# A two-layer diffusion block on one core: the second layer's modulation summed on VectorE in place of TensorE

## The chip, the core and the metric

The kernel runs on one core of one Trainium2 chip. The metric is the device time of one execution in microseconds. A core has a tensor engine (TensorE, in the rows PE; its weight loads have a row of their own, PEld), a vector engine (VectorE, DVE), a scalar engine (ScalarE, ACT), GpSimd (POOL) and SyncE (SP), whose queue here issues nearly all transfers. Each engine works through its own instructions in order and waits for the others by semaphores.

## The reference

Two layers work on 256 latent tokens and 256 context tokens of width 1024. Ahead of each mixer and each feed-forward part the stream is normalised and modulated, and each part's result is gated. Shift, scale and gate come from the conditioning vectors, one for the latents (`c`) and one for the context (`c_ctx`):

```
silu_c  = silu(c);  silu_cc = silu(c_ctx)
m_lat = split(silu_c  @ mod_w[i] + mod_b[i], 6)      # mod_w[i]: 1024 x 6144
m_ctx = split(silu_cc @ mod_w[i] + mod_b[i], 6)
z_lat = modulate(rmsnorm(x, norm1_g[i]), m_lat[0], m_lat[1]) @ w_in[i]
x = x + m_lat[2] * merge(z_lat, att_lat)
x = x + m_lat[5] * ffn(modulate(rmsnorm(x, norm2_g[i]), m_lat[3], m_lat[4]))
```

The feed-forward part is a dense SwiGLU of width 2816 in layer 0 and eight experts, two per token, in layer 1. In the last layer the context only feeds the mixer, so of its modulation only shift and scale of the first norm (`m_ctx[0]`, `m_ctx[1]`) are used.

## The kernel before

**Stages.** Activations lie transposed, 128 features on the partitions and the tokens along the free axis. The order in time is: filters, conditioning and the first modulation (to about 60 us of the profile), mixer of layer 0 with its output projection (to about 320), the dense SwiGLU of layer 0 (to about 710), mixer of layer 1 (to about 870), the experts. A weight block for a matrix multiplication is loaded as 128x1024 floats (`raw`), rounded by ScalarE to `wh` (L262), and VectorE keeps the remainder `wl` (L263). A product is made of three matmuls (L272 to L274), so a block over 512 tokens is 24 matmuls of 128x512 (18 in the last part of the dense stage). `wh` and `wl` have four buffers each, `mm` in PSUM has three, and `raw` has seven, which the modulation's weights (`modw`, tag `raw`, L345) share.

**The modulation** is a vector times a 1024 x 6144 matrix, cut into 12 tiles of 512 output columns (`ct`) for each layer; a tile comes in four chunks (`q`) of 256 rows. For a chunk, `modulation_part` makes four small matmuls (L353): the weights are 32 columns wide (`cvec`: the two conditioning vectors, rest zero) and each goes to its own 32 columns of the array, with 256 columns of `modw` streamed past:

```
for k in range(2):
    for n in range(2):
        g = 64 * k + 32 * n
        self.nc.tensor.matmul(ps[g:g + 32, :L], self.cvec[:, 2 * q + k], w[:, ...], start=q == 0, stop=q == 3, tile_position=(0, g))
```

After the fourth chunk `modulation_row` copies the result out on ScalarE (L360), turns it with two transposes on TensorE (L363), adds its halves on VectorE (L367) and adds the bias (L369). The result is `modT[l]`, with 48 column blocks for both streams.

**Where the chunks stand.** Ten tiles of layer 0 are made in the mixer. The list `chunks` holds the rest: two tiles of layer 0 and all twelve of layer 1, each chunk by itself. `mod_chunk` takes one off the list. It is called in `dense` after each gate or up block but the first three, and in `add_blocks` after each block of the first two of the three parts of the down projection: one chunk after a block of 24 matmuls. The scheduler of the language orders instructions within engines by their dependences from this program order.

**Around it.** Gate times up is made on ScalarE (L890) and VectorE (L891) and split into two parts by `split` (L266, L267); the down projection's result is added to the stream by VectorE in `residual` (L839, once for the latents and once for the context).

Of the kernel before, what the change touches and what calls it, by code (L numbers as in the profile page):

```python
# [18 lines left out]
F32 = mybir.dt.float32  # L19
# [3 lines left out]
OP = mybir.AluOpType  # L23
AX = mybir.AxisListType

P = 128
D = 1024
KD = D // P
L = 256
# [8 lines left out]
PAD = 8  # L38
# [157 lines left out]
class Trunk:  # L196
# [130 lines left out]
    def conditioning(self):  # L327

        nc = self.nc
        lo = self.par_at["c"][0]  # L330
        both = self.pars[:, lo:lo + 2 * KD]
        sc = self.keep.tile([P, 2 * KD], F32, name="silu_c")
        nc.scalar.activation(sc, both, AF.Exp, scale=-1.0)
        nc.vector.tensor_scalar(sc, sc, 1.0, None, op0=OP.add)
        nc.vector.reciprocal(sc, sc)
        nc.vector.tensor_mul(sc, sc, both)
        self.cvec = self.pre.tile([P, KD, 32], F32, name="cvec")
        nc.gpsimd.memset(self.cvec, 0.0)
        for j in range(2):
            nc.vector.tensor_copy(self.cvec[:, :, j], sc[:, j * KD:(j + 1) * KD])  # L340
# [51 lines left out]
    def mod_chunk(self):  # L392

        if not self.chunks:
            return
        l, ct, q = self.chunks.pop(0)
        if q == 0:
            self.mod_ps = self.sc()
        self.modulation_part(self.mod_ps, q, self.modulation_load(l, ct, q))
        if q == 3:  # L400
            self.modulation_row(l, ct, self.mod_ps, self.aux)

    def mod_chunks_until(self, l, ct):
        while self.chunks and self.chunks[0][:2] < (l, ct):
            self.mod_chunk()
# [1037 lines left out]
```

## Time and profile before

| | |
|---|---|
| median of 3 runs | 1789.05 us (1787.66 to 1789.59) |
| the profiled execution | 1784.13 us |
| its span, first to last instruction | 1782.6 us |
| TensorE busy, share of the span | 1682.3 us, 94% |
| VectorE busy | 608.7 us, 34% |
| ScalarE busy | 445.1 us, 25% |
| GpSimd busy | 29.4 us, 2% |

A busy TensorE in these rows is one that has matmuls in flight: records overlap, and their ends are modelled. How long something takes in TensorE's queue is read from the distance of starts. "x8" in a row of the time line means that eight adjacent records were merged. An fp32 matmul leaves two records, so the four small matmuls of a chunk are eight.

### The profile page before, as it was taken

How to read it: one execution, taken by the hardware profiler on the slowest of the kernel's cores; microseconds unless marked ns; L12 is line 12 of the kernel's file. 1: busy time of each engine (PE TensorE's matmuls, PEld its weight loads, DVE VectorE, ACT ScalarE, POOL GpSimd, SP SyncE). 2: the span in 40 equal slices, each digit the busy share in tenths (PEclk: the TensorE clock that was granted, in tenths of full speed). 3: DMA queues.
4: the chain of work that ended last, by engine and by line, in shares of the span. 5: the costliest groups of instructions: out<-in, count | busy, mean ns of one | idle time of the engine just before them, and what ended most of it. 6: DMA issues, size and time to landing. Idle time of an engine off the chain costs nothing. (4 is left out here: it accounts for less than half of the span.)

```text
span 1782.6 us, 27678 instructions
## 1 busy us (share of the span) xinstructions
PE 1682.3 (94%) x11718; PEld 1087.0 (61%) x11718; DVE 608.7 (34%) x1352; ACT 445.1 (25%) x866; POOL 29.4 (2%) x38
## 2 busy tenths in 40 slices
PE   6999999999999999999889999999999999999997
PEld 3877568877777778885755554454545445444443
DVE  5655876423333324778520100311003110031103
ACT  5443564322222123546410000101001000010101
POOL 0021000000000000011000000000000000000000
PEclk9999999999999999999899999999999999999998
DMA  8521353455555553525369999989999899999996
GB/s 311 184 90 44 142 201 95 154 166 165 165 165 166 165 148 113 191 87 195 142 251 367 385 372 412 386 338 403 375 407 425 358 398 370 415 416 397 425 425 261
DMA packets 86313, 475.92 MB, mean 267 GB/s; under 512 B 9707, under 2 KB 13068, under 8 KB 43148
## 3 DMA queue, kind: packets, MB, share of 16 engines
q1 hardware_dynamic: 85580, 473.12, 69.7%
q8 instruction: 121, 1.98, 0.4%
q10 hardware_dynamic: 576, 0.52, 0.1%
q14 instruction: 36, 0.29, 0.0%
HBM read 472.55 MB, written 1.05 MB: 266 GB/s over the span
## 5 line engine op out<-in xcount | busy, mean ns | idle before, releaser
L1136 PE MATMUL mm<-mraw,xg 128*64 128x256 f32 x3584 | 409.5, 382 | 5.2 <-PEq L1192 2.3
L1136 PEld LDWEIGHTS mm<-mraw,xg 128*64 128x64 f32 x3584 | 254.3, 137 | 135.6 <-issue 9.5
L272 PE MATMUL mm<-xh,wh 128*128 128x512 f32 (+1 forms) x656 | 240.6, 368 | 0.8 <-ACT wh L262 0.4
L274 PE MATMUL mm<-xh,wl 128*128 128x512 f32 (+1 forms) x656 | 237.7, 363 | 0.3 <-DVE wl L263 0.3
L273 PE MATMUL mm<-xl,wh 128*128 128x512 f32 (+1 forms) x656 | 237.8, 363 | 0.1
L262 ACT CAST wh<-raw 128x1024 fp32r<-128x1024 f32 (+1 forms) x124 | 128.0, 1034 | 362.5 <-PE mm L273 345.8
L263 DVE TENSOR_TENSOR wl<-raw,wh 128x1024 fp32r<-128x1024 f32 (+1 forms) x124 | 150.1, 1212 | 139.6 <-ACT wh L262 137.9
L272 PEld LDWEIGHTS mm<-xh,wh 128*128 128x128 f32 x656 | 122.9, 188 | 37.2 <-issue 16.5
L274 PEld LDWEIGHTS mm<-xh,wl 128*128 128x128 f32 x656 | 123.2, 188 | 21.7 <-issue 2.2
L273 PEld LDWEIGHTS mm<-xl,wh 128*128 128x128 f32 x656 | 123.0, 188 | 18.9 <-issue 1.5
L1153 DVE TENSOR_TENSOR h<-h,mm 128x256 f32<-128x256 f32 x56 | 23.6, 422 | 320.4 <-ACT h L1152 320.4
L1185 PE MATMUL sc<-mraw,ht 128*64 128x512 f32 x448 | 109.4, 603 | 3.2 <-PEq L1192 1.4
L1185 PE MATMUL mm<-mraw,ht 128*64 128x512 f32 x448 | 108.6, 603 | 3.2 <-PEq L1192 2.1
L1152 ACT ACTIVATE h<-mm 128x256 f32<-128x256 f32 x56 | 21.5, 383 | 344.4 <-PE mm L1136 344.4
L1156 DVE TENSOR_TENSOR hx<-hx,sc 64x256 f32<-64x256 f32 x56 | 23.8, 425 | 242.4 <-ACT hx L1155 242.1
L1155 ACT ACTIVATE hx<-sc 64x256 f32<-64x256 f32 x56 | 21.0, 375 | 288.2 <-PE sc L1147 177.1
L1147 PE MATMUL sc<-mraw,xg 128*32 128x256 f32 x1344 | 76.4, 379 | 0.0
L1164 PE MATMUL aux<-tab_ident,h 128*128 128x128 f32 x112 | 25.1, 302 | 43.7 <-DVE h L1153 43.5
L1185 PEld LDWEIGHTS sc<-mraw,ht 128*64 128x64 f32 x448 | 30.3, 136 | 53.2 <-issue 40.2
L1185 PEld LDWEIGHTS mm<-mraw,ht 128*64 128x64 f32 x448 | 29.0, 136 | 53.9 <-issue 47.1
L1147 PEld LDWEIGHTS sc<-mraw,xg 128*32 128x32 f32 x1344 | 43.4, 110 | 29.2 <-issue 0.8
L1164 PEld LDWEIGHTS aux<-tab_ident,h 128*128 128x128 f32 x112 | 11.5, 140 | 70.2 <-DVE h L1153 64.5
(330 smaller groups left out, 2039.9 us busy)
## 6 DMA issues: line engine op xcount, KB each, us to landing
mraw<-in_eg_dram SPq DMA_DIRECT2D x112, 1024.0 KB, 12.1
mraw<-in_eu_dram SPq DMA_DIRECT2D x112, 1024.0 KB, 15.3
mraw<-in_ed_dram SPq DMA_DIRECT2D x112, 1024.0 KB, 8.6
modw<-in_mod_dram SPq DMA_DIRECT2D x96, 512.0 KB, 3.8
raw<-in_win_dram SPq DMA_DIRECT2D x40, 512.0 KB, 3.9
raw<-in_fg_dram SPq DMA_DIRECT2D x22, 512.0 KB, 4.5
raw<-in_fu_dram SPq DMA_DIRECT2D x22, 512.0 KB, 4.6
raw<-in_wout_dram SPq DMA_DIRECT2D x16, 512.0 KB, 4.4
```

The costliest lines, as they stand in the source:

```text
L262: nc.scalar.copy(hi, raw)
L263: nc.vector.tensor_sub(lo, raw, hi.bitcast(F32))
L272: mm(ps, w[0], x[0], start=start, stop=False)
L273: mm(ps, w[0], x[1], start=False, stop=False)
L274: mm(ps, w[1], x[0], start=False, stop=stop)
L1136: mm(pm[MAIN * j:MAIN * (j + 1), i * L:(i + 1) * L], xg[:, k, :MAIN], r, start=k == 0, stop=k == KD - 1, tile_position=(0, MAIN * j))
L1147: mm(px[q:q + EXTRA], xg[:, k, MAIN:], r, start=k == 0, stop=k == KD - 1, tile_position=(0, q))
L1152: nc.scalar.activation(h, pm[:, :L], AF.Silu)
L1153: nc.vector.tensor_mul(h, h, pm[:, L:])
L1156: nc.vector.tensor_mul(hx[64:], hx[64:], px[64:])
L1164: nc.tensor.transpose(pt[:, f], h[:, f], self.ident)
L1185: mm(pds[e % 2][n * MAIN:(n + 1) * MAIN], ht[:, c:c + MAIN], r[:, at + n * 512:at + (n + 1) * 512], start=ft == 0 and k == 0, stop=ft == N ...
```

## The change

For layer 1, `mod_chunk` calls the new function `mod_sums`. The chunk's weights are loaded as before. VectorE multiplies each half of 128x512 by a column of `silu_c` (one value per partition) and adds it to an accumulator `acc` of 128x512: the first by `tensor_scalar`, the seven others by `scalar_tensor_tensor`. There is one accumulator for the latents and, in the tiles 0 to 3, whose context part is used, one for the context; both use buffers of the tags `pz` and `pa`, which have one buffer each. After the fourth chunk TensorE sums over the partitions, with 128 columns of the accumulator as weights and one column of ones streamed past, four matmuls for an accumulator, and VectorE adds the bias from PSUM. In the tiles 4 to 11 the context's half of `modT` gets the latents' values, and nobody reads it. The matmuls of L353, the copy of L360, the transposes and the reductions are gone for layer 1. Layer 0 is as before.

```diff
+        self.silu_c = sc
...
         l, ct, q = self.chunks.pop(0)
+        if l == 1:
+            return self.mod_sums(ct, q)
         if q == 0:
             self.mod_ps = self.sc()
...
+    def mod_sums(self, ct, q):
+
+
+        nc = self.nc
+        streams = 2 if ct < 4 else 1
+        if q == 0:
+            wide = [self.temps.tile([P, 2, L + 2 * PAD], F32, name=self.name(n), tag=n, bufs=1) for n in ("pz", "pa")[:streams]]
+            self.sums = [t.rearrange("p s t -> p (s t)")[:, :512] for t in wide]
+        w = self.modulation_load(1, ct, q)
+        for k in range(2):
+            wk = w[:, k * 512:(k + 1) * 512]
+            for j, acc in enumerate(self.sums):
+                c = j * KD + 2 * q + k
+                c = self.silu_c[:, c:c + 1]
+                if q == k == 0:
+                    nc.vector.tensor_scalar(acc, wk, c, None, op0=OP.mult)
+                else:
+                    nc.vector.scalar_tensor_tensor(acc, wk, c, acc, op0=OP.mult, op1=OP.add)
+        if q == 3:
+            ps = self.aux(8)
+            for j, acc in enumerate(self.sums):
+                for b in range(4):
+                    nc.tensor.matmul(ps[:, 4 * j + b:4 * j + b + 1], acc[:, b * P:(b + 1) * P], self.ones[:, 0:1],
+                                     start=True, stop=True)
+            m, mb = self.modT[1][:, 4 * ct:4 * ct + 4], self.par("mod_b1")[:, 4 * ct:4 * ct + 4]
+            for j in range(2):
+                at = 4 * j if streams == 2 else 0
+                nc.vector.tensor_add(m[:, :, j], ps[:, at:at + 4], mb)
```

In the rows of the changed kernel, lines behind the new function have moved by 32 (L839 is L871, L891 is L923); the new ones are L421 (first product), L423 (multiply and add), L428 (sum over partitions) and L433 (bias). The transfers on SP's queue stand in the same order in both kernels, and so do all the other matmuls on TensorE.

On TensorE, at the end of the second tile of layer 1, between the last block of the up projection and the first of the down projection (`mm` is the block's result in PSUM, `hy` and `q` are parts of the hidden layer), before:

```order
L273 MATMUL mm_3636<-hy_720_3546,wh_3632 128x512
L274 MATMUL mm_3636<-hy_719_3545,wl_3633 128x512
L353 MATMUL sc_3535<-modw_3661,cvec 32x256 x4
L272 MATMUL mm_3683<-q_623_2987,wh_3679 128x512
L273 MATMUL mm_3683<-q_624_2988,wh_3679 128x512
L274 MATMUL mm_3683<-q_623_2987,wl_3680 128x512
L272 MATMUL mm_3683<-q_632_3032,wh_3679 128x512
L363 MATMUL aux_3669<-tab_ident,t_739_3667 128x128 x2
L273 MATMUL mm_3683<-q_633_3033,wh_3679 128x512
```

and now:

```order
L274 MATMUL mm_3641<-hy_720_3550,wl_3638 128x512
L428 MATMUL aux_3672<-tab_ones,pz_3539 128x1 x4
L428 MATMUL aux_3672<-tab_ones,pa_3540 128x1 x4
L272 MATMUL mm_3691<-q_623_2987,wh_3687 128x512
L273 MATMUL mm_3691<-q_624_2988,wh_3687 128x512
```

The chunk's four matmuls stood behind each of the tile's four blocks, and the transposes a little later; now the eight one-column matmuls stand behind the fourth block alone, and nothing behind the other three.

On VectorE, at the same place, where the next two-stream tile begins (`x_latents`, `x_context` are the two streams, `wl` the remainders of the weight blocks), before:

```order
L839 SCALAR_TENSOR_TENSOR x_latents<-mm_3636,modT_73,x_latents 128x256
L839 SCALAR_TENSOR_TENSOR x_context<-mm_3636,modT_73,x_context 128x256
L263 TENSOR_TENSOR wl_3798<-raw_3795,wh_3797 128x1024
L367 TENSOR_REDUCE modT_74<-aux_3669 128x4 x2
L369 TENSOR_TENSOR modT_74<-modT_74,pars 128x8
L539 SCALAR_TENSOR_TENSOR affa_5651<-modT_74,pars 128x8
L839 SCALAR_TENSOR_TENSOR x_latents<-mm_3683,modT_73,x_latents 128x256
L839 SCALAR_TENSOR_TENSOR x_context<-mm_3683,modT_73,x_context 128x256
```

and now:

```order
L871 SCALAR_TENSOR_TENSOR x_latents<-mm_3641,modT_73,x_latents 128x256
L433 TENSOR_TENSOR modT_74<-aux_3672,pars 128x4 x2
L871 SCALAR_TENSOR_TENSOR x_context<-mm_3641,modT_73,x_context 128x256
L421 TENSOR_SCALAR pz_3716<-modw_3718,silu_c 128x512
L421 TENSOR_SCALAR pa_3717<-modw_3718,silu_c 128x512
L423 SCALAR_TENSOR_TENSOR pz_3716<-modw_3718,silu_c,pz_3716 128x512
L423 SCALAR_TENSOR_TENSOR pa_3717<-modw_3718,silu_c,pa_3717 128x512
L423 SCALAR_TENSOR_TENSOR pz_3716<-modw_3757,silu_c,pz_3716 128x512
L423 SCALAR_TENSOR_TENSOR pa_3717<-modw_3757,silu_c,pa_3717 128x512
L423 SCALAR_TENSOR_TENSOR pz_3716<-modw_3757,silu_c,pz_3716 128x512
L423 SCALAR_TENSOR_TENSOR pa_3717<-modw_3757,silu_c,pa_3717 128x512
L871 SCALAR_TENSOR_TENSOR x_latents<-mm_3691,modT_73,x_latents 128x256
```

Where a remainder `wl` for a later block came right behind the residual update, the first two chunks of the next tile now come, eight operations, and the residual of the following block behind them.

Further on in the same tile on VectorE, before:

```order
L263 TENSOR_TENSOR wl_3845<-raw_3842,wh_3844 128x1024
L839 SCALAR_TENSOR_TENSOR x_latents<-mm_3723,modT_73,x_latents 128x256
L839 SCALAR_TENSOR_TENSOR x_context<-mm_3723,modT_73,x_context 128x256
L263 TENSOR_TENSOR wl_3885<-raw_3882,wh_3884 128x1024
L839 SCALAR_TENSOR_TENSOR x_latents<-mm_3762,modT_73,x_latents 128x256
```

and now:

```order
L423 SCALAR_TENSOR_TENSOR pz_3716<-modw_3796,silu_c,pz_3716 128x512
L423 SCALAR_TENSOR_TENSOR pa_3717<-modw_3796,silu_c,pa_3717 128x512
L423 SCALAR_TENSOR_TENSOR pz_3716<-modw_3796,silu_c,pz_3716 128x512
L423 SCALAR_TENSOR_TENSOR pa_3717<-modw_3796,silu_c,pa_3717 128x512
L263 TENSOR_TENSOR wl_3807<-raw_3804,wh_3806 128x1024
L423 SCALAR_TENSOR_TENSOR pz_3716<-modw_3835,silu_c,pz_3716 128x512
L871 SCALAR_TENSOR_TENSOR x_latents<-mm_3732,modT_73,x_latents 128x256
L871 SCALAR_TENSOR_TENSOR x_context<-mm_3732,modT_73,x_context 128x256
L423 SCALAR_TENSOR_TENSOR pa_3717<-modw_3835,silu_c,pa_3717 128x512
L423 SCALAR_TENSOR_TENSOR pz_3716<-modw_3835,silu_c,pz_3716 128x512
L423 SCALAR_TENSOR_TENSOR pa_3717<-modw_3835,silu_c,pa_3717 128x512
L263 TENSOR_TENSOR wl_3857<-raw_3854,wh_3856 128x1024
```

The first remainder behind the tile's start is `wl_3807`. It belongs to the fourth block after the sum (the three before it, 3691, 3732 and 3771, have theirs by then), and it now stands behind the third chunk.

## Rows read from the trace of the kernel before

**Rows 1.** The page: the span, and each engine's busy time, share and instructions.

```profile
span 1782.6 us, 27678 instructions
...
PE 1682.3 (94%) x11718; PEld 1087.0 (61%) x11718; DVE 608.7 (34%) x1352; ACT 445.1 (25%) x866; POOL 29.4 (2%) x38
```

**Rows 2.** Stretches (us): busy time (count), granted clock, DMA share, GB/s.

```profile
381.70:675.90 294.20, 294.20 (x1509) 213.73 (x1508) 93.68 (x146) 68.74 (x90) 0.00 (x0) 1.00 0.53 161
900.00:1783.00 883.00, 811.19 (x6992) 435.53 (x6992) 131.04 (x353) 90.52 (x215) 0.00 (x0) 0.99 0.94 383
```

**Rows 3.** Waits from 381 to 676 us: total us, times, longest.

```profile
ACT wh L262 <- PE mm L273: 229.8, 47, 5.4
DVE wl L263 <- ACT wh L262: 72.5, 16, 5.0
DVE x_latents L839 <- PE mm L274: 66.5, 16, 4.3
...
PEld sc L353 <- DMA modw<-in_mod_dram: 0.4, 1, 0.4
```

**Rows 4.** Waits of SP's queue from 900 us to the end.

```profile
SPq L1053 <- PE sc L1147: 273.3, 38, 16.9
SPq L1053 <- PEq L1192: 272.3, 32, 13.9
```

**Rows 5.** Time line, TensorE's weight loads around a chunk: start, duration, record.

```profile
451.22 0.19 PEld L273 LDWEIGHTS mm<-hy,wh 128*128 128x128 f32 x1
451.45 0.19 PEld L274 LDWEIGHTS mm<-hy,wl 128*128 128x128 f32 x1
452.00 0.16 PEld L353 LDWEIGHTS sc<-modw,cvec 128*32 128x32 f32 x8 [0.36 <-issue]
452.57 0.19 PEld L272 LDWEIGHTS mm<-q,wh 128*128 128x128 f32 x1 [0.41 <-issue]
...
452.92 0.19 PEld L274 LDWEIGHTS mm<-q,wl 128*128 128x128 f32 x1
```

**Rows 6.** Time line, ScalarE's rounding of successive weights in the first half.

```profile
387.92 1.05 ACT L262 CAST wh<-raw 128x1024 fp32r<-128x1024 f32 x1 [4.73 <-PE mm L273]
394.20 1.05 ACT L262 CAST wh<-raw 128x1024 fp32r<-128x1024 f32 x1 [4.63 <-PE mm L273]
400.71 1.05 ACT L262 CAST wh<-raw 128x1024 fp32r<-128x1024 f32 x1 [4.69 <-PE mm L273]
```

**Rows 7.** Time line, weight loads of one-column matmuls in the filter stage.

```profile
61.33 1.08 PEld L475 LDWEIGHTS sc<-tab_ones,t 128*128 128x128 f32 x8
62.33 0.30 PEld L485 LDWEIGHTS sc<-k,tab_st 128*128 128x128 f32 x2
```

**Rows 8.** Line 475: duration in ns, least, median and greatest; first, last start.

```profile
L475 PE MATMUL sc<-tab_ones,t x32: 167/250/352, 30.5 to 62.2; 128*128 128x1 f32 x32
```

**Rows 9.** Groups of VectorE by shape: busy us, mean ns | idle before.

```profile
L263 DVE TENSOR_TENSOR wl<-raw,wh 128x1024 fp32r<-128x1024 f32 x116 | 142.5, 1230 | 130.7 <-ACT wh L262 129.0
...
L839 DVE SCALAR_TENSOR_TENSOR x_latents<-mm,modT,x_latents 128x256 f32<-128x256 f32 x40 | 18.6, 482 | 95.7 <-PE mm L274 95.7
...
L622 DVE SCALAR_TENSOR_TENSOR e<-e,st 128x512 f32<-128x512 f32 x16 | 11.9, 745 | 0.0
...
L621 DVE TENSOR_SCALAR e<-e,st 128x512 f32<-128x512 f32 x16 | 7.7, 482 | 0.2
...
L369 DVE TENSOR_TENSOR modT<-modT,pars 128x8 f32<-128x8 f32 x24 | 4.0, 165 | 0.6
```

**Rows 10.** The modulation's loads from 380 to 680 us.

```profile
DMA to landing us min/median/max: 3.4/3.7/5.2
```

**Rows 11.** Time line, VectorE's successive instructions behind a down block.

```profile
452.11 0.48 DVE L839 SCALAR_TENSOR_TENSOR x_latents<-mm,modT,x_latents 128x256 f32<-128x256 f32 x1 [4.16 <-PE mm L274]
452.52 0.47 DVE L839 SCALAR_TENSOR_TENSOR x_context<-mm,modT,x_context 128x256 f32<-128x256 f32 x1
...
452.96 1.23 DVE L263 TENSOR_TENSOR wl<-raw,wh 128x1024 fp32r<-128x1024 f32 x1
```

## The prediction

> **What bounds the kernel now.** I read the page's totals first [rows 1], then the busy time by stretch [rows 2], then the waits inside the dense stage [rows 3], and only then single instructions. In the totals the reader is to see one engine, TensorE, busy for 94% of the span, and VectorE for a third of it. That figure alone proves little, since it is a mean over stages, so the stretch of the dense stage with the modulation in it is read by itself: from 381.7 to 675.9 us TensorE is never idle, its granted clock is 1.00 (the 2.4 GHz level), VectorE is busy for 94 of 294 us, ScalarE for 69, and the DMA engines for 0.53 of the time [rows 2]. The waits say who is ahead of whom: ScalarE's rounding of the next weights waits 230 us for TensorE to give a buffer back, VectorE waits for ScalarE and for TensorE's results, and TensorE's own longest wait for data is 0.4 us, once [rows 3]. So in this stage time is what TensorE's queue takes, and an instruction that leaves this queue shortens the program by its whole price, as long as VectorE, which is to take over the work, stays ahead. What follows the stage starts when it ends: in the expert stage too the loads of the weights wait for TensorE, 273 and 272 us in the two largest groups [rows 4], so no transfer there runs by a clock of its own and a gain should come out at the end undiminished.
>
> **What the change removes.** Twelve tiles of layer 1, four chunks each: 48 chunks leave TensorE, and twelve pairs of transposes. A chunk's price is not its busy time but the delay of the weight loads around it. In plain running two weight loads start 0.23 us apart [rows 5]. Across a chunk, from the load of L274 at 451.45 to the next L274 at 452.92, three steps take 1.47 us in place of 0.70: 0.77 us a chunk, of which 0.36 is a gap ahead of its 32-column loads and 0.57 the chunk itself, with a little caught up behind. 48 x 0.77 = 37.0 us. For the transposes, the roundings of successive weights in the first half of the stage start 6.28 us apart with a chunk alone and 6.51 apart with a chunk and a pair of transposes between them [rows 6], so a pair costs 0.23 us and twelve cost 2.8. Together 39.8 us leave the queue. The ScalarE copies and the VectorE reductions of these tiles go as well; both engines wait there, so that counts nothing.
>
> **What it adds to TensorE.** The sum over partitions: for each of the four tiles with both streams 8 matmuls of a 128x128 weight with one column of ones, for each of the eight latent-only tiles 4, in all 4 x 8 + 8 x 4 = 64. The same shape stands in the filter stage: four such matmuls leave eight records, and from the first weight load at 61.33 to the next line's load at 62.33 they take 1.00 us, 0.125 us a record [rows 7]. 64 matmuls are 128 records: 16.0 us. From below the price is bounded by nothing added (the loads hidden behind the running matmuls, as if free); from above by each record costing its median duration of 0.25 us [rows 8], 32 us. I take 16.0, the measured distance of the same form. There is no chunk-like gap in it, for the transposes, which also use the full array, show none: their pair costs 0.23 us in all.
> A rule speaks for the lower end. The Trainium skill, "TensorEngine Tiling (Array Packing)", section Performance Considerations, gives each matmul about 60 cycles and says that one column costs the same as sixty. By that the 128 records would take, as an estimate, 128 x 25 ns (60 cycles at 2.4 GHz) = 3.2 us, and the kernel would gain 36.6 us; by the rows, which hold the 128-column weight load that the rule leaves out, it gains 23.8.
>
> **What it adds to VectorE, and what hides it.** A two-stream tile has 2 multiplications and 14 multiply-adds of 128x512, the one at 0.482 and the other at 0.745 us [rows 9]: 0.96 + 10.43. In the same four blocks it still has four weight remainders at 1.230, eight residual updates at 0.482 (in the up and gate blocks four cheaper operations instead) and two additions of bias of about 0.165 each: 4.92 + 3.86 + 0.33. Sum 20.5 us. TensorE's period for these four blocks becomes 4 x 24 x 0.2333 = 22.4 plus a sum of 2.0, 24.4 us. A latent-only tile has 14.8 us of VectorE work in 23.4. So VectorE has room, 84% and 63%, but it is in order, and the new wait is this: the first multiplication of a tile overwrites the accumulator and must wait until TensorE has read the last one. Behind it in VectorE's queue stand the residual updates of the next block, which free PSUM, and the remainder wl of the block four ahead, which TensorE needs. Walk it from the end of a down block (time 0), in the order shown above: sums end at 2.1, bias, residual and two multiplications to 3.9, six multiply-adds to 8.3, residual of the next block to 9.3, four multiply-adds to 12.3, then wl of block n+4 to 13.5; TensorE wants that one at 2.0 + 3 x 5.6 = 18.8, so 5.3 us are to spare. The last multiply-add ends at 17.4 and TensorE's sum comes at 24.4: 7.0 us to spare. PSUM has three buffers, so a residual update has two blocks' time, 11 us, and is at most some 3 us late. Loads: SP's order is unchanged; a modw buffer is now freed by VectorE, and a weight load may stand behind it. The latest frees at 17.4, the load lands 4 to 5 us later (3.7 in the median for modw, 5.2 at most [rows 10]), and the block is wanted more than 16 us after that. At the change from layer 0 to layer 1 a few VectorE instructions wait for loads that wait for the last old chunks; that costs the remainders behind them some 5 to 7 us once, less than the three blocks of lead. VectorE's part therefore counts nothing; if its cover went, the excess over 24.4 us per tile would come out as TensorE idle time.
> On VectorE's price the rows show that instructions do not hold the engine beyond their records: starts at 452.11, 452.52 and 452.96 for records of 0.48 and 0.47 us [rows 9, 11].
> The Trainium skill, "VectorE: DVE Perf Modes", section The DRAIN you can't avoid, says the opposite, a pause of roughly the duration less 266 ns after each operation. By it a two-stream tile would take about 33 us of VectorE and a latent one 24, an estimate; the stage would lengthen by some 40 us and the kernel end near 1805. By the rows it takes 20.5 and 14.8, and nothing is lost.
>
> **Sum.** 39.8 off, 16.0 on: 23.8 us less. The profiled execution took 1784.13 us for a span of 1782.6, so it would come to 1760.3. It lies 4.9 us under the median of the runs, 1789.05; taken from that median the forecast is 1765.2.
>
> **Rivals.**
> Sums dear: the one-column matmuls do not overlap their weight loads when they stand between the large ones. At 0.25 us a record [rows 8] the gain is 39.8 - 32 = 7.8: 1781. For it: no row shows them between 512-column matmuls. Against it: the measured distance of 0.125.
> Sums free: they cost nothing, 1789.05 - 39.8 = 1749; with the skill's price, 1752. Against it: the same distance.
> The sum waits for VectorE: the last chunk of a tile lands so late that its multiply-adds are exposed, four at 0.745 in a two-stream tile and two in a latent one, 4 x 3.0 + 8 x 1.5 = 24 us, which eats the gain: 1789. It needs the 7 us of spare time gone, thus a load held back by more than a block.
> VectorE becomes the bound (the slower side): each instruction holds the engine longer than its record by a factor x. The kernel is slower by over 0.2%, 3.6 us, when 27.4 us are lost, 4 x (20.5x - 24.4) = 27.4, so from x = 1.52; at x = 5/3 the two-stream tiles lose 9.8 us each and the latent ones 1.3, 49 us, and the time is 1814. For it: sixteen operations in a chain of accumulation that the trace before does not have in this length. Against it: the starts of [rows 11].
>
> **How the numbers follow.** The forecast of 1765 has 0.76, with its own range of 1758 to 1772, mostly the price of a sum (0.1 to 0.17 us a record) and the runs' own spread. Sums dear 0.09, sums free 0.05, the wait that eats the gain 0.05, VectorE the bound 0.05. Within 0.2% (about what a measurement of this kernel can tell from no change) are 1785.5 to 1792.6: the fourth case. Faster 0.90, same 0.05, slower 0.05. The range is 1755 to 1779: the forecast's own, and about half of either sum's case.
>
> **What would show it.** In the changed profile: no L353 records behind the last chunk of layer 0; block starts 5.5 to 5.6 us apart inside a tile; sum groups of about 2.0 and 1.0 us on TensorE, with no wait for VectorE in front; VectorE about 89 us busier (16 multiplications at 0.482 and 112 multiply-adds at 0.745, that is 7.7 + 83.4, with 24 small additions for 36 small operations taken away); the stretch of the 48 chunks shorter by about 24 us and the stages behind it of the same length. Weight loads of TensorE that wait for wl or for a multiply-add would prove me wrong, as would sums spaced by much more or less than 0.125 us a record.

## The result and the profile after

The changed kernel takes 1760.26 us in the median of 4 runs (1757.77 to 1761.25), the kernel before beside it 1789.32 (1787.66 to 1792.14). The ratio is 0.9844, with a 95% interval of 0.9828 to 0.9861: 25 to 31 us less. The profiled execution took 1760.66 us.

The page first. Against [rows 1] TensorE is 23.2 us less busy and VectorE 79.3 us more:

```profile
span 1758.9 us, 27242 instructions
...
PE 1659.1 (94%) x11438; PEld 1097.3 (62%) x11438; DVE 688.0 (39%) x1468; ACT 441.8 (25%) x854; POOL 29.4 (2%) x38
```

The stretches answer to [rows 2] (us, busy time and count of each engine, granted clock, DMA share, GB/s). The part with the modulation is again one in which TensorE is never idle at the full granted clock; VectorE is now busy for 60% of it and not a third. The last 883 us are those of before to within 1.1 us of TensorE's work:

```profile
381.70:652.00 270.30, 270.30 (x1237) 222.57 (x1236) 162.77 (x246) 64.18 (x76) 0.00 (x0) 1.00 0.54 173
...
876.00:1759.00 883.00, 812.32 (x7012) 436.41 (x7010) 131.87 (x355) 91.00 (x216) 0.00 (x0) 0.99 0.94 383
```

The gain is read from ScalarE's rounding of the weights (L262), one record for a block: the same record of the program can be found in both traces. ScalarE waits for TensorE at each, so their distance is TensorE's time for a block. From the first block behind the last chunk of layer 0, 48 blocks on, it is 305.36 us before (375.37 to 680.73) and 279.77 after (378.59 to 658.36): **25.6 us less**. The time line after, start and duration, answers to [rows 6]:

```profile
389.57 1.05 ACT L262 CAST wh<-raw 128x1024 fp32r<-128x1024 f32 x1 [3.95 <-PE mm L273]
395.07 1.04 ACT L262 CAST wh<-raw 128x1024 fp32r<-128x1024 f32 x1 [3.85 <-PE mm L273]
402.36 1.05 ACT L262 CAST wh<-raw 128x1024 fp32r<-128x1024 f32 x1 [5.75 <-PE mm L273]
...
491.01 1.05 ACT L262 CAST wh<-raw 128x1024 fp32r<-128x1024 f32 x1 [3.90 <-PE mm L273]
497.37 1.05 ACT L262 CAST wh<-raw 128x1024 fp32r<-128x1024 f32 x1 [4.81 <-PE mm L273]
```

A block without a sum takes 5.50 us (up and gate; 5.60 in a down block), which is 24 weight loads at 0.23: nothing of the chunk is left. The block with a two-stream sum takes 7.29, with a latent-only sum 6.36, so a sum costs 1.79 and 0.87 us. The weight loads around one of each, in place of [rows 5]:

```profile
394.64 0.19 PEld L274 LDWEIGHTS mm<-xh,wl 128*128 128x128 f32 x1
394.87 1.09 PEld L428 LDWEIGHTS aux<-tab_ones,pz 128*128 128x128 f32 x8
395.88 0.97 PEld L428 LDWEIGHTS aux<-tab_ones,pa 128*128 128x128 f32 x8
396.77 0.19 PEld L272 LDWEIGHTS mm<-xh,wh 128*128 128x128 f32 x1
396.88 0.19 PEld L273 LDWEIGHTS mm<-xl,wh 128*128 128x128 f32 x1
397.12 0.19 PEld L274 LDWEIGHTS mm<-xh,wl 128*128 128x128 f32 x1
...
490.55 0.19 PEld L274 LDWEIGHTS mm<-xh,wl 128*128 128x128 f32 x1
490.77 1.09 PEld L428 LDWEIGHTS aux<-tab_ones,pz 128*128 128x128 f32 x8
491.79 0.19 PEld L272 LDWEIGHTS mm<-xh,wh 128*128 128x128 f32 x1
```

The reader is to see three things: no gap ahead of the sum (394.64 to 394.87 is the usual 0.23, where the step to a chunk's first load took 0.55), 16 records in 1.90 us, and behind them one load that follows after 0.11 in place of 0.23. The waits from 320 to 700 us, as in [rows 3] (total us, times, longest):

```profile
ACT wh L262 <- PE mm L273: 253.3, 60, 6.3
...
DVE modT L433 <- PE aux L428: 26.4, 12, 4.2
...
DVE pz L421 <- PE aux L428: 7.8, 2, 4.2
...
PEld mm L272 <- DVE pa L423: 0.4, 1, 0.4
```

VectorE waits for the sums, 34 us in all: 26.4 for their result and 7.8 for an accumulator to be read. The last row looks like a wait of TensorE for an accumulator and is none: it stands at 366.48 us, behind one of layer 0's chunks, where [rows 5] have the same gap of 0.41 us ahead of the next load. From 378 to 659 us, the 48 blocks, no wait of TensorE stands in the rows. That is how slack looks: the engine with the new work waits, and the one that bounds does not.

### The profile page after: what moved, and what is told of

Read it like the earlier page. It is cut to its first block, busy times and chain, and to the rows that moved or that the text cites. A ratio compares the mean times of both kernels' runs of the same rounds, so it can differ in the third digit from the quotient of the medians.

```text
span 1758.9 us, 27242 instructions
## 1 busy us (share of the span) xinstructions
PE 1659.1 (94%) x11438; PEld 1097.3 (62%) x11438; DVE 688.0 (39%) x1468; ACT 441.8 (25%) x854; POOL 29.4 (2%) x38
## 5 line engine op out<-in xcount | busy, mean ns | idle before, releaser
L274 PE MATMUL mm<-xh,wl 128*128 128x512 f32 (+1 forms) x656 | 237.9, 363 | 0.3 <-DVE wl L263 0.3
L262 ACT CAST wh<-raw 128x1024 fp32r<-128x1024 f32 (+1 forms) x124 | 128.3, 1036 | 340.0 <-PE mm L273 311.6
L274 PEld LDWEIGHTS mm<-xh,wl 128*128 128x128 f32 x656 | 123.1, 188 | 21.8 <-issue 2.2
L1179 PE MATMUL sc<-mraw,xg 128*32 128x256 f32 x1344 | 76.4, 379 | 0.0
L423 DVE SCALAR_TENSOR_TENSOR pz<-modw,silu_c,pz 128x512 f32<-128x512 f32 x84 | 62.8, 747 | 3.1 <-DMA modw<-in_mod_dram 2.1
L1179 PEld LDWEIGHTS sc<-mraw,xg 128*32 128x32 f32 x1344 | 43.4, 110 | 29.2 <-issue 0.8
```

The source lines that it names most:

```text
L262: nc.scalar.copy(hi, raw)
L274: mm(ps, w[1], x[0], start=False, stop=stop)
L423: nc.vector.scalar_tensor_tensor(acc, wk, c, acc, op0=OP.mult, op1=OP.add)
L1179: mm(px[q:q + EXTRA], xg[:, k, MAIN:], r, start=k == 0, stop=k == KD - 1, tile_position=(0, q))
```

## Experiments

The yardstick is the stretch of 48 blocks, since it repeats to 0.05 us from one execution to another of the same kernel, while whole executions differ by several us. For layer0_too and one_pass_sums it leaves out the layer-0 tiles, which lie ahead of it. "Changed" is the changed kernel; times of stretches are from one profile each.

| run | median (us), ratio to before with interval | 48 blocks (us) | against changed |
|---|---|---|---|
| before; again | 1789.32; 1788.33 | 305.36; 305.31 | +25.6 |
| changed | 1760.26, 0.9844 (0.9828 to 0.9861) | 279.77 | |
| quarter_sums | 1782.58, 0.9969 (0.9954 to 0.9985) | 268.98 | -10.8 |
| double_sums | 1784.33, 0.9976 (0.9963 to 0.9989) | 301.93 | +22.2 |
| sums_apart | 1774.12, 0.9914 (0.9896 to 0.9932) | 294.24 | +14.5 |
| old_chunks_too | 1796.40, 1.0041 (1.0025 to 1.0056) | 316.77 | +37.0 |
| latent_only_moved | 1766.85, 0.9879 (0.9863 to 0.9895) | 285.84 | +6.1 |
| double_vector | 1775.79, 0.9928 (0.9908 to 0.9947) | 293.40 | +13.6 |
| layer0_too | 1767.57, 0.9887 (0.9866 to 0.9908) | 279.78 | 0.0 |
| one_pass_sums | 1756.62, 0.9833 (0.9819 to 0.9848) | 270.43 | -9.3 |

**The changed kernel and the kernel before again.** No edit.

> The changed kernel once more, beside the kernel before on the same chip, in five rounds. The first comparison gave 1760.3 against 1789.3 us, 28 to 29 us apart, while the two profiled executions lie 23.7 apart and the dense stage by itself 25.6. Theory (the gain is the dense stage's alone, the rest is spread of the start-up): the difference comes out at 24 to 27 us. Rival (something outside the dense stage gains 3 us as well): it stays at 28 to 30 us.

> The kernel before once more, for a second profile. Its first profiled execution took 1784.1 us, at the low end of its runs (1783.8 to 1792.8). Theory (the runs differ by short falls of the granted clock outside the dense stage, each of 2 to 4 us): the dense stage's first 48 weights behind the last chunk of layer 0 take 305 us again, and where the whole is longer, a stretch with a lower granted clock elsewhere accounts for it. Rival (the dense stage of before itself varies by the 3 us that the medians show beyond the stage's gain): 308 us in the stage.

Measured: 1760.29 us, ratio 0.9841 (0.9823 to 0.9858), 48 blocks in 279.78; before 1788.33 us and 305.31. So the medians stay 27.9 us apart, which is at the edge of the first rival's 28 to 30 and outside the theory's 24 to 27, but the dense stage of neither kernel varies, as the second theory said. The second profiled execution of before took 1788.36 us, 4.2 more than the first, and none of that is in the dense stage: 2.6 us lie ahead of it, where the granted clock was lower in the first 60 us, and 1.6 behind. Some 2 to 3 us of the difference of the medians are thus outside the work that the change touches; why the two kernels' executions differ by them is not settled.

**The price of a sum.** Three runs. In the first, the changed line is

```
-                for b in range(4):
+                for b in range(1):                      # quarter_sums
```

> Of the four one-column matmuls over an accumulator only the first is left, 16 in place of 64; three quarters of layer 1's modulation values are therefore those of the first 128 columns. Theory (each record of a sum costs TensorE's queue 0.11 us, the distance of the weight loads, whatever else runs): 96 records fewer, 10.6 us less than the changed kernel, about 1749.5; a two-stream sum of 1.8 us becomes about 0.45, a latent-only one of 0.88 about 0.22. Rival (the sums hide behind the large matmuls, and the 1.8 us is a fixed price of entering and leaving): no change, within 2 us.

10.8 us less in the 48 blocks, 10.6 expected: a two-stream sum takes 0.47 us, a latent-only one 0.20. The rival of a fixed price falls. The whole kernel is longer, because it computes other modulation values and with them other work for the experts: the matmuls of L1179 in the expert stage ran 1792 times in place of 1344, and the part behind the last rounding took 950 us in place of 913. Its median says nothing of the sums.

```
                 for b in range(4):
-                    nc.tensor.matmul(ps[...], acc[...], self.ones[:, 0:1], start=True, stop=True)
+                    for _ in range(2):                  # double_sums
+                        nc.tensor.matmul(ps[...], acc[...], self.ones[:, 0:1], start=True, stop=True)
```

> Each one-column matmul of a sum is issued twice, 128 in place of 64, with the same result. Theory (0.11 us a record in the queue): 14.2 us more than the changed kernel, about 1774.5, of which each two-stream tile has 1.8 us and each latent-only one 0.88. Rival (a sum is mostly a fixed price): under 4 us more. Rival of the forecast (0.25 us a record when they do not overlap): 32 us more, 1792.

22.2 us more, where 14.2 were expected. The eight latent-only blocks grew by 0.89 us each, as expected; the four two-stream blocks by 4.96, 3.34, 3.32 and 3.36 in place of 1.79. The stretches around the first of them, and one behind the second (columns as above), show why:

```profile
394.00:396.00 2.00, 2.00 (x19) 1.92 (x18) 0.00 (x0) 1.54 (x2) 0.00 (x0) 1.00 0.02 6
396.00:398.00 2.00, 2.00 (x18) 2.00 (x17) 0.49 (x1) 0.00 (x0) 0.00 (x0) 0.84 0.00 0
398.00:400.00 2.00, 2.00 (x6) 1.68 (x7) 1.61 (x5) 0.00 (x0) 0.00 (x0) 0.50 0.03 8
...
404.00:408.00 4.00, 4.00 (x19) 3.31 (x18) 1.18 (x2) 1.47 (x2) 0.00 (x0) 0.98 0.34 127
...
428.00:431.50 3.50, 3.50 (x10) 2.72 (x9) 3.50 (x7) 0.00 (x0) 0.00 (x0) 0.51 0.26 63
```

TensorE was never idle, and yet the granted clock fell to 0.50, the 1.2 GHz level, towards the end of 32 one-column records in a row (weight loads from 394.09 to 398.14), and came back some 7 us later. Behind each of the other three groups it falls too, for some 3.4 us; the 6 us that the next expectation gives for every group holds for the first alone. In the changed kernel, with groups of 16, the granted clock is 1.00 in the whole stage. The next run parts the two causes:

```
+        if q == 1:                                      # sums_apart
+            ps = self.aux(8)
+            for b in range(4 * streams):
+                nc.tensor.matmul(ps[:, b:b + 1], self.ones, self.ones[:, 0:1], start=True, stop=True)
```

> As many extra one-column matmuls as in the run with doubled sums, 64, but on a constant tile and one block after the sum, so that no more than 16 records stand together. In that run the granted clock fell to 0.50 for some 6 us behind each group of 32 records, and the stage grew by 22 us in place of 14. Theory (0.11 us a record, and the excess was the clock's): the stage grows by 14.2 us, with the granted clock at 1.00 throughout. Rival (a record costs 0.17 once there are more of them): 22 us, clock or no clock.

14.5 us more, at a granted clock of 1.00 throughout:

```profile
378.00:480.00 102.00, 102.00 (x509) 85.49 (x508) 65.73 (x105) 20.36 (x24) 0.00 (x0) 1.00 0.47 148
480.00:663.00 183.00, 183.00 (x858) 151.66 (x857) 99.07 (x145) 44.67 (x54) 0.00 (x0) 1.00 0.53 171
```

The same number of matmuls in two groups costs its 0.11 us a record and no more. The 8 us beyond that, with doubled sums, were the clock's: they lie in the four blocks with the low clock, 3.2 us in the first and 1.5 to 1.6 in the others.

**The price of a chunk.** The changed kernel with the old matmuls beside the new path:

```
         w = self.modulation_load(1, ct, q)
+        if q == 0:                                      # old_chunks_too
+            self.mod_ps = self.sc()
+        self.modulation_part(self.mod_ps, q, w)
```

> The changed kernel, and beside its new path the small matmuls of the 48 old chunks as well, into a PSUM tile that nobody reads (no copies, no transposes). Theory (a chunk delays the weight loads by 0.77 us, 0.36 of it ahead of its first load): the dense stage is 48 x 0.77 = 37.0 us longer than in the changed kernel. Rival (a chunk costs what its own records take, 0.57): 27 us longer.

37.0 us more, to the tenth: the gap ahead of the 32-column loads is part of the price, and the records alone (27 us) fall short. The run also adds up against the kernel before: 305.36, plus 14.2 for the sums, less 2.8 for the transposes, which are still gone, is 316.8. VectorE has all its new work here, and no term is left for it: the gain is TensorE's queue.

```
-        if l == 1:
+        if l == 1 and ct >= 4:                          # latent_only_moved
             return self.mod_sums(ct, q)
```

> Only the eight latent-only tiles of layer 1 go over VectorE; the four two-stream tiles stay chunks of small matmuls, as before. Theory (a tile's four chunks 3.08 us and its pair of transposes 0.23, against a sum of 0.88): 8 x 2.43 = 19.4 of the 25.6 us are gained, 6.1 us slower than the changed kernel, and the four two-stream tiles are worth the 6.1. Rival (the gain is one of leaving the other shape of matmul out of the stage altogether, so that a mixture loses most of it): under 12 us are gained.

6.1 us more than changed, in blocks of 6.3 us for the four tiles left alone and 5.5 for the others. The terms add up tile by tile.

**VectorE's room.** Each operation of `mod_sums` on VectorE is followed by the same one into a scratch tile:

```
                     nc.vector.scalar_tensor_tensor(acc, wk, c, acc, op0=OP.mult, op1=OP.add)
+                    nc.vector.scalar_tensor_tensor(extra, wk, c, acc, op0=OP.mult, op1=OP.add)   # double_vector
```

> Each multiplication and multiply-add on VectorE is done a second time into a scratch tile that nobody reads. Theory (VectorE has 20.5 us of work in a two-stream tile of 24.2 and 14.8 in a latent-only one of 23.3, and instructions hold the engine no longer than their records): 14 x 0.747 + 2 x 0.477 = 11.4 us more in a two-stream tile, 31.9, which is 7.7 us too many; four of them, less 7 us of lead once, lengthen the dense stage by 24 to 31 us; 5.7 us more in a latent-only tile give 20.5 and cost nothing, so the blocks of those tiles stay 5.5 to 5.6 us apart. Rival (VectorE has far more room than the sum says): nothing changes. Rival (each instruction holds the engine 5/3 of its record): the latent-only tiles are late too, by some 8 to 10 us each.

13.6 us more. The roundings show it in two distances of 12.7 and 13.0 us in place of 5.6, behind the second and the third two-stream sum; the latent-only tiles took the changed kernel's time. The place is right and the size is not. VectorE's part had been summed from durations, but its records overlap. In the changed kernel's time line (start, duration)

```profile
406.99 0.74 DVE L423 SCALAR_TENSOR_TENSOR pz<-modw,silu_c,pz 128x512 f32<-128x512 f32 x1
407.65 0.74 DVE L423 SCALAR_TENSOR_TENSOR pa<-modw,silu_c,pa 128x512 f32<-128x512 f32 x1
408.32 0.74 DVE L423 SCALAR_TENSOR_TENSOR pz<-modw,silu_c,pz 128x512 f32<-128x512 f32 x1
```

multiply-adds of 0.74 us start 0.66 apart. A two-stream tile fills VectorE for 17.7 to 18.5 us of 24.0, a latent-only one for 12.9 of 22.9. Doubled, the first comes to about 18.2 + 14 x 0.66 + 2 x 0.40 = 28.2, an estimate, 4.2 too many; four tiles less the 7 us of lead give 10 us. How a late VectorE reaches TensorE is seen in TensorE's own waits in this run, the only ones of its matmuls from 378 to 480 us but for a second one for a remainder `wl`:

```profile
435.89 0.76 PE L272 MATMUL mm<-q,wh 128*128 128x512 f32 x1 [2.77 <-DVE x_context L874]
437.59 0.80 PE L274 MATMUL mm<-q,wl 128*128 128x512 f32 x1 [0.51 <-DVE wl L263]
...
467.44 0.77 PE L272 MATMUL mm<-xh,wh 128*128 128x512 f32 x1 [3.56 <-DVE x_context L874]
```

and in VectorE's queue just ahead of the first:

```profile
434.60 0.74 DVE L426 SCALAR_TENSOR_TENSOR rz<-modw,silu_c,pz 128x512 f32<-128x512 f32 x1
435.26 0.48 DVE L874 SCALAR_TENSOR_TENSOR x_context<-mm,modT,x_context 128x256 f32<-128x256 f32 x1
```

The residual update of the context stands behind four of the multiply-adds (432.62 to 435.26), and it frees the `mm` buffer that TensorE's next block needs. So TensorE stands still twice, for 6.3 us in all, and a remainder that comes late adds 1.0. Behind each of the two the granted clock falls as well (matmul records of 0.76 us for 0.39; mean granted clock 0.93 from 378 to 480 us), and that is about the rest of the 13.6 us. The prediction had named this path, the residual updates that free PSUM, and had given it 11 us of room. ScalarE waits longer still, up to 11.7 us for a weight block, since the loads share the `raw` buffers with the modulation's and stand in SP's queue until VectorE gives one back; but no wait of TensorE for ScalarE's `wh` stands in the rows of this stretch, so that wait isn't what costs. In the changed kernel SP's queue waits for VectorE too, from 378 to 480 us 41 us for one multiply-add's buffers (total, times, longest)

```profile
SPq L259 <- DVE pa L423: 41.1, 9, 7.6
```

but there the block lands before ScalarE asks for it: no wait of L262 for a load stands among the waits of its dense stage.

**More of it.** Layer 0's two tiles in the stage go the same way, by the same call for both layers:

```
-        if l == 1:
-            return self.mod_sums(ct, q)
...
+        self.mod_sums(l, ct, q)                         # layer0_too
```

> The two tiles of layer 0 that are computed in the dense stage go the same way, over VectorE. Theory (chunk 0.77 us, pair of transposes 0.23, two-stream sum 1.79): 8 x 0.77 + 2 x 0.23 - 2 x 1.79 = 3.0 us less than the changed kernel, about 1757, with the first two tiles' blocks 5.5 us apart inside a tile. Rival (VectorE is late there, since at the start of the stage the lead of the weights is small and its queue is fuller): no gain, or a loss of 1 to 5 us, with TensorE waiting for wl or for an accumulator in the first 60 us of the stage.

The rival was right that it is a loss, and wrong about the place. Inside the dense stage the moved tiles gain 1.8 us (nine blocks in 49.55 for 51.35), but ahead of it 6.4 are lost (from the seventh rounding to the 35th 254.2 us, in the changed kernel 247.9). There VectorE has the residual updates, the sums of squares and the norm between two stages, on which TensorE waits. Of the first moved tile's sixteen operations fifteen stand among them from 281 to 299 us, where VectorE in the changed kernel waits for TensorE twice, for 2.5 and 5.1 us. First the changed kernel, then this one, whose time line runs 2.8 us ahead up to there: the last residual updates of the context, its sums of squares and the first operation of the norm.

```profile
308.20 0.48 DVE L871 SCALAR_TENSOR_TENSOR x_context<-sc,modT,x_context 128x256 f32<-128x256 f32 x1
308.60 0.42 DVE L551 TENSOR_TENSOR ssq<-ssq,t 128x256 f32<-128x256 f32 x1
308.93 1.22 DVE L263 TENSOR_TENSOR wl<-raw,wh 128x1024 fp32r<-128x1024 f32 x1
311.07 0.42 DVE L282 TENSOR_SCALAR rv<-aux 128x256 f32<-128x256 f32 x1 [0.92 <-ACT ry L281]
```

```profile
307.66 1.26 DVE L865 SCALAR_TENSOR_TENSOR x_context<-sc,modT,x_context 128x256 f32<-128x256 f32 x3
308.84 0.41 DVE L545 TENSOR_TENSOR ssq<-ssq,t 128x256 f32<-128x256 f32 x1
309.17 1.22 DVE L263 TENSOR_TENSOR wl<-raw,wh 128x1024 fp32r<-128x1024 f32 x1
310.30 0.41 DVE L545 TENSOR_TENSOR ssq<-ssq,t 128x256 f32<-128x256 f32 x1
310.64 0.74 DVE L417 SCALAR_TENSOR_TENSOR pa<-modw,silu_c,pa 128x512 f32<-128x512 f32 x1
312.53 0.42 DVE L282 TENSOR_SCALAR rv<-aux 128x256 f32<-128x256 f32 x1 [1.15 <-ACT ry L281]
```

With the 2.8 us taken off, the last residual update is 3 us late, and a weight remainder now stands ahead of the last sum of squares and not behind it: that sum is 4.5 us later and the norm 4.3. TensorE waits for the normed stream and for ScalarE's work on a gate block (the changed kernel's rows have no wait over 0.4 us of its matmuls here), and between the two waits its granted clock is low, where the changed kernel has 1.00:

```profile
316.38 0.62 PE L272 MATMUL mm<-xh,wh 128*128 128x256 f32 x3 [1.19 <-ACT xh L587]
...
329.17 0.50 PE L272 MATMUL mm<-xh,wh 128*128 128x512 f32 x1 [2.22 <-ACT t L916]
```

```profile
318.00:321.00 3.00, 3.00 (x16) 3.00 (x16) 3.00 (x10) 1.74 (x5) 0.00 (x0) 0.50 0.00 0
```

An operation that costs nothing in one stage costs its price in the next. The stretches account for 4.6 us; the median lies 7.3 above the changed kernel's, and the profiled execution was the fastest of the four, so the rest stays open.

**A version that takes both lessons** moves only the second of the two layer-0 tiles, and lets the last multiply-add write a type that TensorE multiplies in one pass:

```
-        if l == 1:
+        if l == 1 or ct == 11:                          # one_pass_sums
...
+                    out = acc
+                    if q == 3 and k == 1:
+                        out = self.tmp(("rz", "rv")[j], 1, 512, F32R)
+                        rounded.append(out)
-                    nc.vector.scalar_tensor_tensor(acc, wk, c, acc, op0=OP.mult, op1=OP.add)
+                    nc.vector.scalar_tensor_tensor(out, wk, c, acc, op0=OP.mult, op1=OP.add)
...
-                    nc.tensor.matmul(ps[:, 4 * j + b:4 * j + b + 1], acc[...], self.ones[:, 0:1], ...)
+                    nc.tensor.matmul(ps[:, at:at + 2], rounded[j][...], self.one_r, ...)
```

> A version meant to beat both: the last multiply-add of each accumulator writes its result rounded to the type that TensorE takes in one pass, so that a sum's matmul leaves one record in place of two (its moving operand is two columns wide); and the second of layer 0's two tiles in the dense stage goes over VectorE as well, the first stays as it was, since with both the norm ahead of the stage was late by 5 us. Theory (0.11 us a record): 64 records fewer, 7.1 us, and for the layer-0 tile 4 x 0.77 + 0.23 - 0.9 = 2.4 us; together 9.5 us under the changed kernel, about 1751. Rival (a sum is priced by its matmuls, not by its records): 2 us under it, about 1758.

> The version with one-pass sums and one layer-0 tile moved, again, beside the changed kernel on the same chip. Its first profile shows 11.8 us less in the dense stage than the changed kernel, but 8.5 us more behind it, where the granted clock fell once more among the experts (some 3 us) and was low for longer in the last 20 us (some 4 us); the medians were only 3.7 us apart. Theory (those falls come and go from one execution to the next): the dense stage is again 11.8 us shorter, and the medians of this call lie 5 to 12 us apart. Rival (this kernel always meets them): they are there again in the profile, and the medians lie 2 to 5 us apart.

> The changed kernel beside the run above. Theory: 1760 us, the dense stage's 48 weights 279.8 us, for both theories.

In the dense stage it does a little more than the 9.5 us expected: a two-stream sum takes 0.87 us and a latent-only one 0.40, half of the changed kernel's, as the theory of a price by records has it; the layer-0 tile gains 2.5; and the down blocks take 5.44 us in place of 5.60, for which I have no reason. Together 11.8 us, in both of its profiles (48 blocks in 270.43 twice, and 2.5 us ahead of them). The kernel as a whole gains less. Run side by side with the changed kernel, it took 1755.81 us (1755.55 to 1758.86; ratio 0.9829, 0.9811 to 0.9846) and the other 1758.85 (1758.60 to 1763.97; 0.9850, 0.9827 to 0.9873; 48 blocks in 279.77): 3.0 us, with intervals that overlap. It beats the kernel before surely, the changed one probably. The rival was right that the losses are there again. Both its profiles have, among the experts, a pause that the changed kernel has too, but with another sequel. First its rows, a matmul behind the pause and the stretches from there; then the changed kernel's:

```profile
1319.53 0.38 PE L1138 MATMUL aux<-back,ye 96*128 96x256 f32 x1 [1.28 <-ACT ye L267]
```

```profile
1321.00:1328.00 7.00, 7.00 (x30) 3.53 (x30) 1.17 (x3) 0.37 (x1) 0.00 (x0) 0.53 1.01 418
```

```profile
1332.32 0.38 PE L1130 MATMUL aux<-back,ye 96*128 96x256 f32 x1 [1.28 <-ACT ye L267]
```

```profile
1334.00:1341.00 7.00, 7.00 (x54) 4.35 (x50) 2.71 (x7) 0.37 (x1) 0.00 (x0) 1.00 1.01 428
```

The same 1.28 us of pause, and in the one kernel the granted clock falls to half for some 7 us, in the other it stays. That makes 3.0 us (between the same two records of the expert stage 72.0 us and 68.9). double_sums, old_chunks_too, latent_only_moved and quarter_sums have it too; before, changed, sums_apart, layer0_too and double_vector don't. What decides is not settled. My expectation also put 4 us down to a low clock in the last 20 us; the trace doesn't bear that out, the clock there is alike in both, and what differs in the first of the two profiles is TensorE waiting 2.1 us for a weight load of the experts, at 1707 us, and a granted clock of 0.66 in the mixer of layer 1 (800 to 820 us), where the same part of the changed kernel beside it had 0.74. What is left over in each, some 2 to 3 us, is not traced.

## Why the prediction was right

Forecast 1765.2 us, measured 1760.3; in the profile the forecast of 1760.3 stands against 1760.66, which is closer than its terms deserve, as two errors cancel: the sums cost 1.8 us less than forecast, and 1.9 us were lost outside the stage in these two executions, which the forecast could not know.

- **What leaves TensorE, 39.8 us.** Confirmed: 37.0 for the chunks by old_chunks_too, and in latent_only_moved a pair of transposes still takes 0.22 to 0.24 (6.52 for 6.28).
- **What comes onto TensorE, 16.0 us.** Measured, 4 x 1.79 + 8 x 0.88 = 14.2. The term mis-sized is the price of a record: 0.125 from [rows 7] is the whole way to the next line's load, as here (1.90 us for 16), but the load behind that one then follows after 0.11 in place of 0.23. Worked out as the prediction did it for a chunk, from the load of L274 at 394.64 to the next at 397.12, a sum costs 2.48 - 0.70 = 1.78 us, 0.11 a record. 39.8 - 14.2 = 25.6, which is the stretch's gain. The rival "sums dear" falls by quarter_sums and sums_apart, "sums free" by the same. The records of L428 do last 0.25 us in the median, as in [rows 8], but they overlap, so their duration was never a price:

```profile
L428 PE MATMUL aux<-tab_ones,pz x96: 164/250/250, 395.1 to 652.7; 128*128 128x1 f32 x96
```

- **VectorE counts nothing.** Confirmed; its load was put too high, at 20.5 us a two-stream tile in place of about 18.2 and at 89 us in all in place of 79.3, by summing durations as if they did not overlap. [Rows 11] had shown the overlap (starts 0.41 apart for records of 0.48), and the working used it only against a slower VectorE.
- **The wait for the accumulator** falls on VectorE, as said (7.8 us), and does not reach TensorE in the 48 blocks.
- **The stages behind** are unchanged [rows 2]. The 23.7 us between the two spans are 25.6 less in the 48 blocks, 3.2 more before the dense stage (in the first 60 us the granted clock was 0.89 in place of 0.94, ahead of any changed instruction), and 1.3 less behind. The forecast took the two executions as alike there.
- **From the profile to the median** the forecast added the 4.9 us by which that execution lay under its median. Before's second profile shows what such a difference is made of, stretches of a lower granted clock outside the dense stage. The changed kernel's profile lies 0.4 us above its median, so the 4.9 did not carry over. Of the 4.9 us between forecast and result 1.8 are the sums' lower price; the other 3.1 are this difference between the executions of the two kernels, whose cause stays open.

The Trainium skill, "TensorEngine Tiling (Array Packing)", section Performance Considerations, has one column cost a matmul the same as sixty, some 60 cycles, which is 25 ns as an estimate at 2.4 GHz; 0.11 us a record disagrees. The Trainium skill, "TensorE: Matmul & The Clock Gate", section LDWEIGHTS (loading the stationary operand), gives a weight load columns / 1.2 in ns, as an estimate 107 ns for 128 columns, and the 0.11 us measured here agrees. So a matmul with one column seems to be priced by its weights; no run varies their width. The Trainium skill, "VectorE: DVE Perf Modes", section The DRAIN you can't avoid, has a pause after each operation, and none is seen: multiply-adds of 0.74 us start 0.66 us apart. The same section adds that a next operation which is not held starts earlier, and the trace agrees with that; the prediction had set the pause against the rows without this sentence.

## What to carry to other kernels

Price a small matmul between large ones by the distance of the weight loads around it, gap and catching-up included; neither its busy time nor its column count says it. Moving work to an engine with room is free as long as what else stands in that engine's queue still comes in time: look at the buffers that it gives back to the bounding engine, here PSUM's behind the residual updates, and at the places where it is itself waited for, as at a norm between two stages. Compare versions by a stretch between two records that both have, since whole executions here differ by more than a small edit is worth.

## What the hardware showed that was not expected

- The granted clock fell to 0.50 while TensorE was without a pause, at the end of or behind each of four groups of 32 one-column records, and at none of 16; it cost 1.5 to 3.2 us each time.
- One pause of 1.28 us ahead of the same matmul is followed by 7 us at half clock in some kernels and not in others, at 3 us a time. Of 11.8 us won in the dense stage by the last version, only about 3 were left at the end.
- The operands' type sets the number of records of a matmul, one with both operands rounded (fp32r) and two in fp32, and records set the price: 0.11 us each, 8 for a two-stream sum in one pass and 16 otherwise.
